# Two state products of an rwkv chain, in halves of the array's columns, and Gram products of two heads by turns

## The chip, the cores and the metric

The kernel runs on one core of one Trainium2 chip. The core has five engines: TensorE (PE, matrix products, with its weight loads shown as PEld), VectorE (DVE), ScalarE (ACT), GpSimd (POOL) and SyncE (SP, here only a DMA queue). The metric is the device time of one execution in microseconds; the lower the better. A profiled execution gives, for every instruction, when it began and how long it took.

## The reference

Two transformer-like blocks over 256 positions and 2048 channels. The second block sends one input projection through three branches (a gated delta rule "gdn", an "rwkv7" scan, an "s5" scan) and merges them. The change is in the rwkv7 branch, whose heart is this scan over positions, for 16 heads of 64 channels:

```
def step(state, xs):
    r_t, w_t, k_t, v_t, kk_t, a_t = xs
    sa = jnp.einsum('bhvk,bhk->bhv', state, -kk_t)
    state = (state * w_t[:, :, None, :] + sa[..., None] * (kk_t * a_t)[:, :, None, :]
             + v_t[..., None] * k_t[:, :, None, :])
    return state, jnp.einsum('bhvk,bhk->bhv', state, r_t)
```

## The kernel before

The big projections are float32 products, split into two parts of a shorter format (`split`, L167 and L124) and multiplied in three passes (`wh` and `wl` are the parts of the weights; the result tile is `pj`). Their weights stream from HBM through SP's queue, ACT and DVE prepare them, and PE multiplies. Nearly all of PE's time is theirs.

The rwkv scan is done in chunks of 64 positions. `rwkv` works on a group of four heads (index `q`, four groups), and each group goes through these steps:

- Gram products. For each head the products of its (64 channels x 128) operands `BK` and `KR`, both held in `G8`, for four chunks: a matrix with 64 rows (contracted) and 128 columns as weights. The heads of a pair lie on the upper and the lower 64 partitions, so on the upper and lower half of the array's rows. DVE masks the results into `U`, `W` (tile `o0`) and `E` (tile `E8`). After each head the generator yields `LAT["prod"]`.
- `inverse64`: a triangular inverse `AT` of each chunk, through two DMA round trips, DVE steps and four sets of 64x64 products (`e,d` and `c,d` in the trace), by turns on the array's upper left and lower right quarter.
- The chain over four chunks `c`. `p1` multiplies `W` with the state tile `ST` (tile `a4`: the state in its upper 64 rows, the values `v` in its lower 64), `p2` multiplies the inverse, `p3` multiplies `E` with the state; DVE and ACT carry the results from step to step. `W`'s lower right quarter (rows 64 to 127, columns 64 to 127) is zero, set by a memset on POOL.

All of this is a generator that runs beside the projections: `mm` adds an estimated time to `K.clock` for every product, and `tick`, called between the products of a projection, resumes a generator when the clock has passed its last yield (the table `LAT`, in microseconds). A second generator holds the s5 branch. Afterwards the framework's scheduler sets the final order on each engine; PE then runs strictly in the given order, so a small product whose operand is late holds up the projections behind it. The result tiles of this generator come from a ring of three PSUM buffers (`K.ps()`).

In the trace a float32 product shows as two instructions of each kind (two weight loads, two products); a projection's as one. Names are tile names without numbers: `ps<-a,o` is `p1` (moving `a4`, weights `o0`), `ps<-a,E` is `p3`, `ps<-G,AT` is `p2`, `ps<-G` are the Gram products, `ps<-s5x,ct` the read-out of the s5 branch (on 32 columns at a time), `ps<-e,bonw` a small product ahead of the Gram ones.

Of the kernel before, what the change touches and what calls it, by code (L numbers as in the profile page):

```python
# [25 lines left out]
LAT = dict(small=12.0, turn=2.5, bc=8.5, fd=10.0, fb=1.2, fh=0.8, z=0.3, sm=8.85, pt=1.42, st=6.0, ix=0.55, top=9.0, s5=11.0, inv=34.0, pr=1.3,  # L26
           prz=1.6, feat=15.0, prod=2.2, c1=1.25, c3=1.3, gn=11.0, sc=6.5, conv=22.5, ln=4.1, rw=2.3, rb=9.0, gp=1.0,
           kt=1.0, gu=3.25, gc=1.3, gR=1.5, go=1.0, gg=7.2)
# [887 lines left out]
class Block2:  # L916
# [263 lines left out]
    def rwkv(self, pl, q, f, wl, al, rn, prm, C):  # L1180
        K, nc = self.K, self.nc
# [49 lines left out]
        KR, BK = G8[:, 0], G8[:, 1]  # L1231
# [15 lines left out]
        p = K.ps()  # L1247
# [6 lines left out]
        W = K.t(self.po, [128, 4, 4, 128], "o0")  # L1254
        E = K.t(pl, [128, 4, 4, 128], "E8")
        U = K.t(pl, [128, 8, 64], "h2")
        ST = K.t(pl, [128, 4, 4, 64], "a4")
        PC = K.t(pl, [64, 4, 4], "PC")
        nc.gpsimd.memset(W[64:128, :, :, 64:128], 0.0)
        nc.gpsimd.memset(ST[0:64, 0], 0.0)  # L1260
        for j in range(2):
            nc.vector.tensor_copy(PC.rearrange("p (i j) c -> p i j c", j=2)[:, :, j], E3[64 * j:64 * j + 64, :, :, 64])
        for i in range(2):
            for j in range(2):
                h = 2 * i + j
                rows = slice(64 * j, 64 * j + 64)
                p = K.ps()
                pv = p.rearrange("p (c t) -> p c t", c=4)
                for c in range(4):
                    K.mm(pv[:, c], BK[rows, i, c].rearrange("p a t -> p (a t)"),  # L1270
                         KR[rows, i, c].rearrange("p a t -> p (a t)"))
                ms = lambda rw, m: C["ms"][rw].unsqueeze(1).to_broadcast([64, m, 64])
                lo, hi = slice(0, 64), slice(64, 128)
                for d in range(2):
                    K.tt(U[64 * d:64 * d + 64, 2 * h:2 * h + 2], pv[lo, d::2, 0:64], ms(lo, 2), ALU.mult)
                K.tt(W[hi, h, :, 0:64], pv[hi, :, 0:64], ms(hi, 4), ALU.mult)
                K.tt(E[:, h, :, 64:128], pv[:, :, 64:128], C["mi"].unsqueeze(1).to_broadcast([128, 4, 64]), ALU.mult)
                nc.scalar.copy(W[0:64, h], KR[rows, i].rearrange("p c a t -> p c (a t)"))
                yield LAT["prod"]
            p = K.ps()  # L1280
            for c in range(4):
                K.tr(p[:, c * 128:c * 128 + 128], BK[:, i, c].rearrange("p a t -> p (a t)"))
            pv = p.rearrange("p (c j n) -> p c j n", c=4, j=2)
            for j in range(2):
                nc.scalar.copy(E[:, 2 * i + j, :, 0:64], pv[:, :, j])
            p = K.ps()
            for c in range(4):
                K.tr(p[0:64, c * 128:c * 128 + 128], v[:, i, c * 64:c * 64 + 64])
            nc.scalar.copy(ST[64:128, :, 2 * i:2 * i + 2], p[0:64].rearrange("p (c j n) -> p c j n", c=4, j=2))
# [8 lines left out]
        hv = lambda p: p[:, 0:256].rearrange("p (h s) -> p h s", h=4)  # L1298
        for c in range(4):
            d = c % 2  # L1300
            rows = slice(64 * d, 64 * d + 64)
            p1 = K.ps()
            for h in range(4):
                K.mm(hv(p1)[:, h], W[:, h, c], ST[:, c, h])
            nc.vector.tensor_copy(X0[rows], hv(p1)[0:64])
            nc.scalar.copy(Y0[64:128], hv(p1)[64:128])
            if c < 3:
                pcb = PC[:, :, c:c + 1].to_broadcast([64, 4, 64])
                K.tt(mp, ST[0:64, c], pcb, ALU.mult)
            yield LAT["c1"]  # L1310
            p2 = K.ps()
            for h in range(4):
                K.mm(hv(p2)[0:64, h], AT[rows, 2 * h + c // 2], X0[rows, h])
            nc.vector.tensor_copy(ST[0:64, c], hv(p2)[0:64])
            yield LAT["c1"]
            p3 = K.ps()
            for h in range(4):
                K.mm(hv(p3)[:, h], E[:, h, c], ST[:, c, h])
            if c < 3:
                K.tt(tm, hv(p3)[0:64], pcb, ALU.mult)  # L1320
                K.tt(ST[0:64, c + 1], tm, mp, ALU.add)
            K.tt(Y[rows, c // 2], hv(p3)[64:128], Y0[64:128], ALU.add)
            yield LAT["c3"]
# [16 lines left out]
        p = K.ps()  # L1340
# [552 lines left out]
```

## Time and profile before

| what | value |
|---|---|
| time, median of 3 runs | 2163.0 us (2161.22 to 2163.57) |
| profiled execution, its own time | 2168.05 us |
| its span, first to last instruction | 2166.3 us |
| PE busy, share of the span | 2120.1 us, 98% |
| DVE, ACT, POOL busy | 77%, 48%, 2% |
| mean granted TensorE clock | 0.994 of full speed |

The profiled execution took 5.05 us longer than the median of the runs; 1.75 us of it lie outside its span. PE works nearly all the time and the other engines have room; where PE stands idle it waits for DVE or ACT. A busy PE is not PE at its peak: how close the starts of its instructions stand tells more than how long each one lasts, since they overlap.

### The profile page before, as it was taken

The numbers are of one execution on the slowest core, as the hardware profiler recorded it, in microseconds if no ns is written. First come the engines' busy times: TensorE is split into PE (matmuls) and PEld (weight loads), VectorE is DVE, ScalarE is ACT, GpSimd is POOL, SyncE is SP. The second block draws the span as 40 slices with busy tenths as digits, with TensorE's granted clock in tenths as the row PEclk, the third lists the DMA queues.
The fourth block names the chain that finished last, engine by engine and source line by source line (L and its number), as shares of the span: only waits on it lengthen the run. The fifth ranks groups of instructions, "written<-read, shape, count | busy, mean of one in ns | idle before, by whom it ended". The sixth has DMA issues, their size and how long they took to land. (4 is left out here: it accounts for less than half of the span.)

```text
span 2166.3 us, 32785 instructions
## 1 busy us (share of the span) xinstructions
PE 2120.1 (98%) x12275; PEld 1790.6 (83%) x12275; DVE 1668.8 (77%) x2919; ACT 1043.2 (48%) x1498; POOL 49.4 (2%) x113
## 2 busy tenths in 40 slices
PE   9999999999999999999999999999999999999998
PEld 8888888888898888888888788767778868888786
DVE  6788866667999876665789998988998857866565
ACT  5445454544454455555544444434446635644344
POOL 2001000000000000000000000000000000000000
PEclk9999999999999999999999999999999999999999
DMA  8666656767666766876686686676765675795674
GB/s 255 194 183 175 174 147 184 241 205 224 198 183 204 209 171 181 280 215 200 196 233 199 186 242 191 195 225 181 211 202 165 197 219 176 235 300 156 210 232 152
DMA packets 356143, 440.09 MB, mean 203 GB/s; under 512 B 50380, under 2 KB 262528, under 8 KB 355664
## 3 DMA queue, kind: packets, MB, share of 16 engines
q1 hardware_dynamic: 328240, 430.81, 65.6%
q10 hardware_dynamic: 26512, 4.68, 1.2%
q0 software_dynamic: 1232, 2.51, 0.4%
q8 instruction: 96, 1.57, 0.3%
q14 instruction: 63, 0.52, 0.1%
HBM read 396.35 MB, written 41.57 MB: 202 GB/s over the span
## 5 line engine op out<-in xcount | busy, mean ns | idle before, releaser
L167 ACT CAST wh<-raw 128x1024 fp32r<-128x1024 f32 (+4 forms) x668 | 683.8, 1026 | 860.2 <-PE pj L141 708.7
L124 DVE TENSOR_TENSOR wl<-raw,wh 128x1024 fp32r<-128x1024 f32 (+4 forms) x668 | 794.0, 1191 | 336.6 <-ACT wh L167 327.5
L141 PE MATMUL pj<-x,wh 128*128 128x512 f32 (+3 forms) x3008 | 1017.8, 387 | 0.7 <-ACT wh L167 0.7
L141 PE MATMUL pj<-x,wl 128*128 128x256 f32 (+2 forms) x2864 | 805.8, 281 | 2.3 <-DVE wl L124 2.3
L141 PEld LDWEIGHTS pj<-x,wh 128*128 128x128 f32 (+2 forms) x3008 | 553.2, 187 | 125.7 <-issue 9.1
L141 PEld LDWEIGHTS pj<-x,wl 128*128 128x128 f32 (+2 forms) x2864 | 539.1, 188 | 8.7 <-issue 4.0
L141 PE MATMUL pj<-wh,x 128*128 128x512 f32 (+2 forms) x1472 | 452.3, 383 | 0.0
L141 PEld LDWEIGHTS pj<-wh,x 128*128 128x128 f32 x1472 | 272.4, 189 | 49.0 <-issue 6.0
L141 PE MATMUL pj<-wl,x 128*128 128x512 f32 (+2 forms) x736 | 280.1, 381 | 0.9 <-DVE wl L124 0.9
L141 PEld LDWEIGHTS pj<-wl,x 128*128 128x128 f32 x736 | 139.0, 189 | 25.7 <-DVE wl L124 2.2
L141 PE MATMUL pj<-wh,y 128*128 128x512 f32 x512 | 158.3, 390 | 0.0
L141 PEld LDWEIGHTS pj<-wh,y 128*128 128x128 f32 x512 | 95.9, 188 | 19.8
L141 PE MATMUL pj<-wl,y 128*128 128x512 f32 x256 | 99.9, 390 | 0.0
L141 PE MATMUL pj<-wh,E 128*128 128x512 f32 x192 | 78.6, 409 | 2.8 <-ACT wh L167 2.3
L141 PE MATMUL pj<-wl,E 128*128 128x512 f32 x192 | 77.0, 402 | 1.9 <-DVE wl L124 1.8
L141 PE MATMUL pj<-wh,G 128*128 128x512 f32 x192 | 77.3, 403 | 0.0
L124 DVE TENSOR_TENSOR raw<-y 128x256 f32<-128x256 f32 (+7 forms) x256 | 64.0, 289 | 3.0
L141 PEld LDWEIGHTS pj<-wl,y 128*128 128x128 f32 x256 | 48.1, 188 | 9.9
L124 DVE TENSOR_TENSOR y<-raw 128x128 f32<-128x128 f32 (+7 forms) x256 | 46.2, 223 | 2.6
L141 PEld LDWEIGHTS pj<-wh,E 128*128 128x128 f32 x192 | 37.1, 193 | 12.0 <-ACT wh L167 3.2
L141 PEld LDWEIGHTS pj<-wl,E 128*128 128x128 f32 x192 | 37.0, 193 | 10.9 <-DVE wl L124 3.5
L141 PEld LDWEIGHTS pj<-wh,G 128*128 128x128 f32 x192 | 37.2, 194 | 8.0 <-issue 0.2
(457 smaller groups left out, 1997.4 us busy)
## 6 DMA issues: line engine op xcount, KB each, us to landing
raw<-in_w_in_dram SPq DMA_DIRECT2D x460, 512.0 KB, 3.8
raw<-in_w_out_dram SPq DMA_DIRECT2D x96, 512.0 KB, 4.7
raw<-in_w_branch_dram SPq DMA_DIRECT2D x48, 512.0 KB, 4.5
raw<-in_w_in_dram SPq DMA_DIRECT2D x24, 344.0 KB, 3.2
s5t<-y SPq DMA_DIRECT2D x16, 512.0 KB, 6.2
s5tb<-s5t SPq DMA_DIRECT2D x32, 256.0 KB, 3.7
raw<-in_w_in_dram SPq DMA_DIRECT2D x16, 384.0 KB, 3.6
gates<-ev SPq DMA_DIRECT2D x12, 512.0 KB, 3.7
```

The lines of the kernel that those rows point to most:

```text
L124: return (eng or self.nc.vector).tensor_tensor(out=out, in0=a, in1=b, op=op)
L141: i = self.nc.tensor.matmul(out, l, r, start=st, stop=sp, **k)
L167: i = self.nc.scalar.copy(h, src)
```

## The change

The Gram products of the two heads of a pair are now issued by turns, chunk by chunk, into two result tiles that are taken from the ring together; one yield of twice the old length follows instead of one after each head. `p1` comes as two products per head: `W`'s left 64 columns with all 128 rows, and its right 64 columns with the upper 64 rows only (the lower ones were zero; the memset is gone). `p3` comes as two products per head on the left and the right 64 columns, both with all 128 rows.

```diff
-        nc.gpsimd.memset(W[64:128, :, :, 64:128], 0.0)
         nc.gpsimd.memset(ST[0:64, 0], 0.0)
...
         for i in range(2):
-            for j in range(2):
+
+            pvs = [K.ps().rearrange("p (c t) -> p c t", c=4) for _ in range(2)]
+            for c in range(4):
+                for j, pv in enumerate(pvs):
+                    rows = slice(64 * j, 64 * j + 64)
+                    K.mm(pv[:, c], BK[rows, i, c].rearrange("p a t -> p (a t)"),
+                         KR[rows, i, c].rearrange("p a t -> p (a t)"))
+            for j, pv in enumerate(pvs):
                 h = 2 * i + j
                 rows = slice(64 * j, 64 * j + 64)
-                p = K.ps()
-                pv = p.rearrange("p (c t) -> p c t", c=4)
-                for c in range(4):
-                    K.mm(pv[:, c], BK[rows, i, c].rearrange("p a t -> p (a t)"),
-                         KR[rows, i, c].rearrange("p a t -> p (a t)"))
...
-                yield LAT["prod"]
+            yield 2 * LAT["prod"]
...
             for h in range(4):
-                K.mm(hv(p1)[:, h], W[:, h, c], ST[:, c, h])
+                K.mm(hv(p1)[0:64, h], W[:, h, c, 0:64], ST[:, c, h])
+                K.mm(hv(p1)[64:128, h], W[0:64, h, c, 64:128], ST[0:64, c, h])
...
             for h in range(4):
-                K.mm(hv(p3)[:, h], E[:, h, c], ST[:, c, h])
+                for d in (0, 64):
+                    K.mm(hv(p3)[d:d + 64, h], E[:, h, c, d:d + 64], ST[:, c, h])
```

First place: PE at the first chunk's `p1` in the first group of heads. Before (a row is one product and its count; the size is that of its output, partitions x columns):

```order
L141 MATMUL pj_11046<-x_8492,wh_11049 128x512
L141 MATMUL pj_11046<-x_8492,wl_11050 128x256
L141 MATMUL ps_1796_11062<-a_1681_10320,o_1678_10317 128x64 x4
L141 MATMUL pj_11046<-x_8492,wh_11049 128x512
L141 MATMUL pj_11046<-x_8492,wl_11050 128x256
```

and now:

```order
L141 MATMUL pj_11045<-x_8492,wh_11048 128x512
L141 MATMUL pj_11045<-x_8492,wl_11049 128x256
L141 MATMUL ps_1796_11061<-a_1681_10320,o_1678_10317 64x64 x8
L141 MATMUL pj_11045<-x_8492,wh_11048 128x512
L141 MATMUL pj_11045<-x_8492,wl_11049 128x256
```

Four products became eight in one piece with nothing between them; of the eight every second has 64 instead of 128 rows of weights, by the code above. `p3` reads the same, with `E` for `o`, and all 32 runs of `p1` and `p3` stand in one piece as here.

Second place: PE at the first Gram products, in the first group of heads. Before (`ps_1683` is the first head's result; the second head's four products follow 14 projection products later):

```order
L141 MATMUL ps_1676_10312<-e_1652_10143,bonw_10070 128x256 x2
L141 MATMUL ps_1683_10326<-G_1653_10147 128x128 x4
L141 MATMUL pj_10299<-x_8492,wh_10302 128x512
L141 MATMUL pj_10299<-x_8492,wl_10303 128x256
L141 MATMUL pj_10299<-x_8492,wh_10302 128x512
```

and now, both heads' results `ps_1683` and `ps_1684`:

```order
L141 MATMUL ps_1676_10312<-e_1652_10143,bonw_10070 128x256 x2
L141 MATMUL ps_1683_10325<-G_1653_10147 128x128
L141 MATMUL ps_1684_10326<-G_1653_10147 128x128
L141 MATMUL ps_1683_10325<-G_1653_10147 128x128
L141 MATMUL ps_1684_10326<-G_1653_10147 128x128
L141 MATMUL ps_1683_10325<-G_1653_10147 128x128
L141 MATMUL ps_1684_10326<-G_1653_10147 128x128
L141 MATMUL ps_1683_10325<-G_1653_10147 128x128
L141 MATMUL ps_1684_10326<-G_1653_10147 128x128
L141 MATMUL pj_10299<-x_8492,wh_10302 128x512
```

The second head's products moved up between the first head's.

Third place: PE at the second pair of heads in the third group (`ps_2196` and `ps_2200` are the two heads). Before:

```order
L141 MATMUL ps_2196_13341<-G_2147_13076 128x128 x4
L141 MATMUL pj_13479<-wh_13635,x_8492 128x512 x2
L141 MATMUL pj_13479<-wl_13636,x_8492 128x512
L141 MATMUL pj_13479<-wh_13635,x_8492 128x512 x2
L141 MATMUL pj_13479<-wl_13636,x_8492 128x512
L141 MATMUL pj_13479<-wh_13635,x_8492 128x512
L141 MATMUL ps_2200_13371<-G_2147_13076 128x128 x4
```

and now (`ps_2193` and `ps_2194`):

```order
L141 MATMUL ps_2192_13376<-ident_75,c_2120_13007 64x128 x4
L141 MATMUL pj_13540<-wh_13660,x_8492 128x512 x2
L141 MATMUL pj_13540<-wl_13661,x_8492 128x512
L141 MATMUL pj_13540<-wh_13660,x_8492 128x512
L141 MATMUL ps_2193_13382<-G_2144_13118 128x128 x4
L141 MATMUL pj_13540<-wh_13678,x_8492 128x512
L141 MATMUL ps_2194_13383<-G_2144_13118 128x128 x4
L141 MATMUL pj_13540<-wl_13679,x_8492 128x512
```

Here the scheduler did not keep the turns: the heads still stand apart. So it is in the second pair of the second, third and fourth group; the other five of the eight pairs stand by turns. In the first pair of those three groups the two heads' runs already stood next to each other before, one head after the other.

## Rows read from the trace of the kernel before

**Rows 1.** The page's busy time of each engine over the whole span.

```profile
PE 2120.1 (98%) x12275; PEld 1790.6 (83%) x12275; DVE 1668.8 (77%) x2919; ACT 1043.2 (48%) x1498; POOL 49.4 (2%) x113
```

**Rows 2.** Windows summed: 1130-1180, 1309-1347, 1460-1495, 1607-1648 us, where the chunk chains run.

```profile
sum 164.00, PE 163.92 PEld 137.06 DVE 139.79 ACT 70.63 POOL 3.56; mean PE 40.98 PEld 34.26 DVE 34.95 ACT 17.66 POOL 0.89
```

**Rows 3.** Groups by line and shape: rows*columns of weights, xcount | busy us, mean ns.

```profile
L141 PE MATMUL ps<-a,o 128*128 128x64 f32 x128 | 16.7, 273 | 0.1
L141 PE MATMUL ps<-G 64*128 64x128 f32 x128 | 16.7, 285 | 0.4 <-DVE E L124 0.4
L141 PE MATMUL ps<-a,E 128*128 128x64 f32 x128 | 16.1, 269 | 0.0
```

**Rows 4.** Timeline of PE at one p2 and one p1: start us, us, what.

```profile
1136.11 0.39 PE L141 MATMUL pj<-x,wh 128*128 128x512 f32 x1
1136.42 0.68 PE L141 MATMUL ps<-G,AT 64*64 64x64 f32 x8
1137.03 0.38 PE L141 MATMUL pj<-x,wl 128*128 128x256 f32 x1
1137.25 0.40 PE L141 MATMUL pj<-x,wh 128*128 128x512 f32 x1
...
1140.59 0.39 PE L141 MATMUL pj<-x,wh 128*128 128x512 f32 x1
1140.82 0.27 PE L141 MATMUL pj<-x,wl 128*128 128x256 f32 x1
1140.93 1.00 PE L141 MATMUL ps<-a,o 128*128 128x64 f32 x8
1141.74 0.47 PE L141 MATMUL pj<-x,wh 128*128 128x512 f32 x1
1142.05 0.28 PE L141 MATMUL pj<-x,wl 128*128 128x256 f32 x1
```

**Rows 5.** Timeline of PE at products of the inverse, by turns on two quarters.

```profile
1121.64 1.15 PE L141 MATMUL ps<-e,d 64*64 64x64 f32 x32
1122.72 0.50 PE L141 MATMUL pj<-x,wh 128*128 128x512 f32 x1
```

**Rows 6.** Timeline of PE where tiles of two shapes follow each other directly.

```profile
1480.06 0.62 PE L141 MATMUL ps<-s5x,ct 128*32 128x256 f32 x2
1480.61 0.67 PE L141 MATMUL ps<-G,AT 64*64 64x64 f32 x8
1481.21 1.07 PE L141 MATMUL ps<-s5x,ct 128*32 128x256 f32 x10
1482.22 0.50 PE L141 MATMUL pj<-wl,x 128*128 128x512 f32 x1
```

**Rows 7.** Timeline of PE at Gram products: one head alone, then two heads' runs adjacent.

```profile
1063.18 1.02 PE L141 MATMUL ps<-e,bonw 128*128 128x256 f32 x4
1064.13 1.16 PE L141 MATMUL ps<-G 64*128 64x128 f32 x8
1065.22 0.50 PE L141 MATMUL pj<-x,wh 128*128 128x512 f32 x1
1065.55 0.28 PE L141 MATMUL pj<-x,wl 128*128 128x256 f32 x1
...
1528.73 1.71 PE L141 MATMUL ps<-G 64*128 64x128 f32 x16
1530.37 0.50 PE L141 MATMUL pj<-wh,x 128*128 128x512 f32 x1
```

**Rows 8.** Timeline of PE in the gdn branch: last score products, first product of the inverse.

```profile
1935.06 1.02 PE L141 MATMUL ps<-E 128*128 128x256 f32 x4
1935.73 0.47 PE L141 MATMUL pj<-x,wl 128*128 128x256 f32 x1
...
1979.92 1.15 PE L141 MATMUL ps<-e,d 64*64 64x64 f32 x32 [1.06 <-DVE e L1158]
```

**Rows 9.** Windows near the end: length, busy us of each engine, granted clock.

```profile
2018.00:2036.00 18.00, 13.60 (x44) 9.72 (x43) 6.91 (x8) 6.11 (x14) 1.01 (x1) 0.81 0.72 233
```

## The prediction

> **What bounds the kernel now.** I read the page's busy line first: PE works 98% of the span, DVE 77%, POOL 2% [rows 1]. That is an average, so I then asked for the busy time in the four stretches in which the chunk chains of the four groups run (`p1`, `p2`, `p3`): PE is busy 163.92 of 164.00 us there, DVE 139.79 [rows 2]. In these stretches PE sets the pace and stands nowhere idle, so what a run of small products takes or gives back there goes into the time in full; the projections queue behind it. The groups by line say how much there is to win: `p1`, `p3` and the Gram products are 128 instructions each, 16 to 17 us of busy time each [rows 3]. More than some 20 us cannot come from making them shorter. Last, the timeline tells what one run costs, measured by when the next product starts.
>
> **Price of a run now.** `p1` is eight instructions on the whole array. A projection product with 512 columns holds PE 0.23 us (1140.59 to 1140.82), one with 256 columns 0.11 (to 1140.93), and `p1` starts with no delay. It holds PE 0.81 us, and the product behind it 0.31 instead of 0.23 [rows 4]. So 0.81 + 0.08 = 0.89 us a run, 0.11 an instruction.
>
> **Price of a run on part of the array.** `p2` is eight instructions on one 64x64 quarter. The product ahead should have ended at 1136.34, `p2` starts at 1136.42, holds PE 0.61 us, and the 256-column product behind it takes 0.22 instead of 0.11 [rows 4]: 0.08 + 0.61 + 0.11 = 0.80 us. The inverse's 32 instructions by turns on two quarters hold PE 1.08 us [rows 5]. If two run at a time they are 16 steps against `p2`'s 8, so 8 steps cost 1.08 - 0.61 = 0.47 us, 0.059 a step, and 0.14 us of a run is fixed. Not overlapped, 24 more instructions would cost 0.02 each, which nothing near it does; I take them as overlapped.
>
> What is the fixed part paid for? Where `p2` stands directly between two pieces of the s5 read-out, which uses 128x32 tiles, it still holds PE 0.60 us (1480.61 to 1481.21), and the two read-out instructions ahead 0.55 [rows 6]. So the price is not that of coming from the whole array or going back to it: a change between two shapes of tile, 64x64 and 128x32, costs 0.60 - 0.47 = 0.13 us as well. The same place shows that column groups with all 128 rows do overlap: ten 256-column instructions take 1.01 us, while on the whole array four take 0.95 [rows 6, 7].
>
> The Trainium skill has a rule for this: "Mode switching requires drain: Changing tiling mode (not just tile) drains the TensorE" (TensorEngine Tiling (Array Packing), Key Properties), and its list of modes has 128x64 and 64x64 as different ones. The rows above agree as far as they go, with 0.13 us a change; no row shows these two shapes side by side.
>
> **p1 after.** Its eight products are, head by head, one with 128 rows x 64 columns of weights and one with 64 x 64. Both halves lie on different columns, but their shapes differ, so the shape changes eight times a run. If each change costs what it costs in rows 6, a product (two instructions) takes 2 x 0.059 + 0.13 = 0.25 us, eight take 2.0, and with 0.08 ahead and 0.11 behind the run costs 2.19 us against 0.89: +1.30. There are 16 runs: +20.8 us. Bounds: if the shapes don't matter and the halves overlap, the run is 8 steps in one piece and costs `p2`'s 0.80, -0.09 x 16 = -1.4 us. If the two instructions of a product also came apart, 16 changes, 16 x 0.19 + 0.19 = 3.2 us, +37 us. I take 20.8, since `p2` between two pieces of another shape is the nearest row.
>
> **p3 after.** Both halves have 128 rows x 64 columns, one shape. By turns they are 8 steps, 0.80 us against 0.89: -0.09 x 16 = -1.4 us. If they did not overlap, 16 steps, 0.94 + 0.14 + 0.19 = 1.27, +6 us; the ten overlapping instructions of rows 6 speak against that.
>
> **Gram products after.** A head alone costs PE 1.09 us from 1064.13, 0.10 more in the product behind, and about 0.09 ahead (four 256-column instructions of about 0.215 should have ended at 1064.04): 1.28. Two heads' runs next to each other hold PE 1.64, only 0.55 more than one: the row halves do overlap once the second head's come into sight [rows 7]. By turns from the start, both heads should hold PE as one does, 1.09. In the first group two pairs save a whole run each, 2 x 1.28 = 2.6 us; in the first pair of the other groups the runs were adjacent already, 3 x 0.55 = 1.7; the second pairs of those groups are still apart (third place in the order), nothing. Sum -4.2 us; bounds 0 (no overlap) and -5 (the price ahead and behind counted again).
>
> **What I count at nothing.** The memset on POOL, which is busy 2% [rows 1]. DVE's and ACT's work on the results: the same instructions. The longer yield: the second head's results are there earlier than before. In the first group's second pair the second result tile is that of the transposes, so one head waits for two copies on ACT; 0.2 us, once.
>
> **What moves besides.** The estimated clock runs 0.64 us faster per chunk (a product with 64 output columns counts 0.107 us with 128 rows, half that with 64), and the scheduler rearranges later work. Most of it stays within a few products, but one place is larger. Before, 237 projection products stood between the last score products of the second gdn half and its inverse, and the inverse still came 1.06 us late, 44.2 us after 1935.73 [rows 8]. Now 167 stand there, 103 of 512 and 64 of 256 columns, 103 x 0.23 + 64 x 0.117 = 31.2 us: PE could wait 9 to 13 us. Against that the end of that chain comes earlier before the last branch (134 products instead of 54), where PE loses 4.4 us of 18 to waits and the granted clock falls to 0.81 [rows 9]: 6 to 8 us may come back. The first half's inverse has 180 products instead of 150, 2 to 4 us the better. I set the sum at 0, +-8.
>
> **Sum.** 20.8 - 1.4 - 4.2 + 0.2 = +15.4. PE idles 46.2 us in the whole span [rows 1], some of it behind these chains for DVE, which gains time when PE is later: I take off 2. That is +13.4 us on the profiled execution's 2168.05 (span 2166.3 and 1.75 around it), 2181.4; on the runs, whose median is 5 us lower, 2163.0 + 13.4 = 2176.
>
> **Rivals.**
> A. Shape costs nothing where the tiles touch no common part of the array. The two halves of `p1` share no column; in rows 6 the tiles may. Then -1.4 - 1.4 - 4.2 + 0.2 = -6.8 us, 2156: not slower. It decides if a run of `p1` holds PE under 0.9 us. For it: the inverse's quarters, which share neither rows nor columns, overlap fully [rows 5]. Against it: every change of shape in the rows carries the 0.13. Beside it stands a page of the Trainium skill (TensorE: Matmul & The Clock Gate, Part 3, The mechanism), by which each instruction names its row and column groups and tiles that don't conflict overlap; it would have `p1` as this rival does.
> B. As forecast, and the inverse of the second gdn half is late as well, with nothing given back at the end: +13.4 + 10 = 2186. For it: 31.2 us of work where 44.2 were needed [rows 8]. Against it: the gain behind it.
> C. The weights of the next shape are loaded while the last one still runs, so that half of the 0.13 is hidden: 8 x 0.19 + 0.19 = 1.7 a run, +13 for `p1`, +6 in all, 2169. Against it: `p2`'s first step in rows 6 hides nothing.
>
> **How the numbers follow.** Forecast 0.52, A 0.25, B 0.13, C 0.10. Runs of this kernel spread about 0.1%, so I call anything within 0.2% (4.3 us) no change: 2158.7 to 2167.3. With +-8 us of rearrangement, forecast and B are slower nearly always, C a bit over half, A faster in two of three. Slower 0.65, same 0.13, faster 0.22. The range takes in B and most of A: 2152 to 2188; the forecast's own is 2167 to 2185.
>
> **What would show it.** A `p1` run should hold PE about 2.0 us, with eight pieces 0.25 apart; a `p3` run about 0.6 with its instructions in pairs of nearly equal start; the first Gram run 16 instructions in 1.1 us; the four chain stretches together 19 us longer with the same number of projection products. It is wrong if `p1` holds PE under 1 us (rival A), or if PE's waits near the two gdn inverses differ by over 8 us from before.

## The result and the profile after

The changed kernel takes 2178.22 us (median of 4 runs, 2176.53 to 2179.41) against 2163.28 for the kernel before; the ratio is 1.0067, 95% interval 1.0052 to 1.0082. It is slower by 14.9 us, where the prediction said 13.4 and gave 2176. The profiled execution took 2179.41 us, its span is 2177.6.

The page's busy time of each engine, after:

```profile
PE 2132.2 (98%) x12531; PEld 1791.1 (82%) x12531; DVE 1670.3 (77%) x2919; ACT 1045.8 (48%) x1498; POOL 48.9 (2%) x109
```

Against [rows 1] PE is busy 12.1 us longer, with 256 more instructions, and idles 2177.6 - 2132.2 = 45.4 us instead of 46.2. So the loss is work on PE, not waiting.

The groups by line and shape, after; the columns are those of [rows 3]:

```profile
L141 PE MATMUL ps<-a,o 128*64 128x64 f32 x128 | 21.0, 246 | 0.0
L141 PE MATMUL ps<-a,o 64*64 64x64 f32 x128 | 20.8, 242 | 0.0
L141 PE MATMUL ps<-G 64*128 64x128 f32 x128 | 12.8, 284 | 1.4 <-DVE E L124 1.4
L141 PE MATMUL ps<-a,E 128*64 128x64 f32 x256 | 11.0, 228 | 0.0
```

`p1` went from 16.7 to 41.8 us of busy time, `p3` from 16.1 to 11.0, the Gram products from 16.7 to 12.8; the wait ahead of the Gram products from 0.4 to 1.4. One run of each kind in the timeline of PE, after (start us, length us, and what; neighbours in time are merged into one row):

```profile
1129.99 0.28 PE L141 MATMUL pj<-x,wl 128*128 128x256 f32 x1
1130.20 2.12 PE L141 MATMUL ps<-a,o 128*64 128x64 f32 x16
1132.25 0.50 PE L141 MATMUL pj<-x,wh 128*128 128x512 f32 x1
...
1135.86 0.28 PE L141 MATMUL pj<-x,wl 128*128 128x256 f32 x1
1136.07 0.69 PE L141 MATMUL ps<-a,E 128*64 128x64 f32 x16
1136.68 0.50 PE L141 MATMUL pj<-x,wh 128*128 128x512 f32 x1
```

The `x16` of the first run covers both shapes (the row names only the first). It holds PE 1132.25 - 1130.20 = 2.05 us: eight products, 0.256 us apart. With what it costs ahead and behind the median run takes 2.25 us, against the 0.89 of [rows 4]. `p3` has as many instructions on as many columns and holds PE 0.61 us (0.81 with both ends). Its two halves have one shape, `p1`'s have two. The first Gram products, after:

```profile
1061.98 1.02 PE L141 MATMUL ps<-e,bonw 128*128 128x256 f32 x4
1062.93 1.16 PE L141 MATMUL ps<-G 64*128 64x128 f32 x16
1064.02 0.50 PE L141 MATMUL pj<-x,wh 128*128 128x512 f32 x1
...
1070.79 1.25 PE L141 MATMUL ps<-G 64*128 64x128 f32 x16 [0.46 <-DVE E L124]
1071.97 0.39 PE L141 MATMUL pj<-x,wl 128*128 128x256 f32 x1
```

Two heads by turns hold PE 1.09 us, what one head alone took in [rows 7]. The second pair waits 0.46 us for a mask step on DVE; by the code such steps read, and so free, the result tiles of the ring.

### The profile page after: what moved, and what is told of

Same layout as the page of the kernel before. It is cut to its first block, busy times and chain, and to the rows that moved or that the text cites. A ratio compares the mean times of both kernels' runs of the same rounds, so it can differ in the third digit from the quotient of the medians.

```text
span 2177.6 us, 33290 instructions
## 1 busy us (share of the span) xinstructions
PE 2132.2 (98%) x12531; PEld 1791.1 (82%) x12531; DVE 1670.3 (77%) x2919; ACT 1045.8 (48%) x1498; POOL 48.9 (2%) x109
## 5 line engine op out<-in xcount | busy, mean ns | idle before, releaser
L141 PEld LDWEIGHTS pj<-x,wl 128*128 128x128 f32 (+2 forms) x2864 | 539.5, 188 | 12.8 <-DVE wl L124 5.6
L124 DVE TENSOR_TENSOR y<-raw 128x128 f32<-128x128 f32 (+7 forms) x256 | 46.2, 223 | 2.5
L124 DVE TENSOR_TENSOR s5w<-ps,s5tb 128x512 f32<-128x512 f32 x64 | 42.8, 684 | 2.5 <-PE ps L141 2.3
```

The lines of the kernel that those rows point to most:

```text
L124: return (eng or self.nc.vector).tensor_tensor(out=out, in0=a, in1=b, op=op)
L141: i = self.nc.tensor.matmul(out, l, r, start=st, stop=sp, **k)
```

## The experiments

PE busy and idle are those of one profiled execution; "p1 run" is the median of the runs that stand between two projection products, with the delays they cause ahead and behind. The kernel before, run beside them, took 2163.89 (median) beside the first four experiments, 2161.32 beside the next four and 2163.05 (one run) beside the last two.

| kernel | median us | ratio to before, 95% interval | p1 run us | PE busy us | PE idle us |
|---|---|---|---|---|---|
| before | 2163.28 | 1 | 0.89 | 2120.1 | 46.2 |
| after | 2178.22 | 1.0067 (1.0052 to 1.0082) | 2.25 | 2132.2 | 45.4 |
| p1 whole | 2162.89 | 1.0000 (0.9990 to 1.0011) | 0.89 | 2111.8 | 47.1 |
| p1 in one shape | 2155.64 | 0.9957 (0.9945 to 0.9969) | 0.81 | 2104.5 | 45.5 |
| p1 left, then right | 2165.50 | 1.0006 (0.9997 to 1.0015) | 1.41 | 2117.7 | 47.0 |
| p1 alone | 2183.95 | 1.0086 (1.0072 to 1.0099) | 2.25 | 2136.2 | 46.1 |
| clock count alone | 2160.62 | 0.9994 (0.9981 to 1.0007) | 0.89 | 2115.3 | 43.4 |
| Gram alone | 2165.82 | 1.0005 (0.9991 to 1.0018) | 0.89 | 2111.8 | 44.9 |
| p3 alone | 2168.64 | 1.0028 (1.0016 to 1.0040) | 0.89 | 2123.1 | 52.3 |
| one shape, and a pause | 2146.55 | 0.9923 (0.9907 to 0.9938) | 0.81 | 2101.8 | 44.4 |
| disjoint, two shapes | 2181.72 (1 run) | | 2.23 | 2134.8 | 45.1 |
| disjoint, one shape | 2157.45 (1 run) | | 0.81 | 2109.7 | 46.0 |

**p1 whole again.** In the changed kernel:

```diff
-                K.mm(hv(p1)[0:64, h], W[:, h, c, 0:64], ST[:, c, h])
-                K.mm(hv(p1)[64:128, h], W[0:64, h, c, 64:128], ST[0:64, c, h])
+                K.mm(hv(p1)[:, h], W[:, h, c], ST[:, c, h])
```

> The changed kernel with p1 on the whole array again (and the memset of W's zero quarter back); p3 and the Gram products stay changed. Main theory (a change between the tile shapes 128x64 and 64x64 costs about 0.13 us, eight times a p1 run): the whole loss goes, a p1 run costs 0.89 us again, the sum is 2163 - 1.4 (p3) - 4.2 (Gram) = 2157, with 8 us either way for the rearrangement of the later work. Rival R (the loss is the rearrangement of work around the inverses, p1 is a bystander): 2170 or more.

The loss is gone (0.9990 to 1.0011), so `p1` made it and rival R fell. But the 5.6 us that `p3` and the Gram products should have brought don't show either; 2162.9 lies inside the 8 us allowed, at its far side.

**p1 in two products of one shape.**

```diff
-                K.mm(hv(p1)[0:64, h], W[:, h, c, 0:64], ST[:, c, h])
-                K.mm(hv(p1)[64:128, h], W[0:64, h, c, 64:128], ST[0:64, c, h])
+                for d in (0, 64):
+                    K.mm(hv(p1)[d:d + 64, h], W[:, h, c, d:d + 64], ST[:, c, h])
```

> The changed kernel with p1 still in two products a head by turns, but both with all 128 rows (the lower rows of the right half are zero again, by the memset), so that all have the shape 128x64. Main theory (the price is the change of shape): a run becomes eight steps in pairs like p3, 0.80 us instead of 2.25, and the time is 2163 - 1.4 - 1.4 - 4.2 = 2156, 8 us either way. Rival D (the price is that of more, smaller products by turns on two column halves, whatever their shape): a run stays near 2.2 us and the time at 2178. Rival R (rearrangement): 2170 or more.

2155.64, as the main theory said. The number of products and the columns they use are the changed kernel's; the right halves have 64 rows of zeros more. Its run in the timeline of PE:

```profile
1127.66 0.28 PE L141 MATMUL pj<-x,wl 128*128 128x256 f32 x1
1127.87 0.69 PE L141 MATMUL ps<-a,o 128*64 128x64 f32 x16
1128.48 0.50 PE L141 MATMUL pj<-x,wh 128*128 128x512 f32 x1
```

0.61 us on PE instead of 2.05, by doing more arithmetic. Rival D fell: turns and halves cost nothing by themselves. The stretch from the first `p1` to behind the last `p3` of the first group of heads, which holds 180 projection products before, after and with one shape, says the same in windows (columns: length, then busy us and count for PE, PEld, DVE, ACT and POOL, granted clock, DMA share, GB/s). Before, after, and with one shape:

```profile
1133.82:1179.19 45.37, 45.37 (x302) 38.30 (x301) 39.04 (x65) 18.66 (x27) 0.95 (x1) 1.00 0.69 206
```

```profile
1130.20:1180.78 50.58, 50.58 (x366) 39.51 (x365) 39.28 (x66) 18.77 (x27) 0.00 (x0) 1.00 0.60 178
```

```profile
1127.87:1172.76 44.89, 44.89 (x365) 35.63 (x364) 39.01 (x66) 18.65 (x27) 0.95 (x1) 1.00 0.69 202
```

The last two are 5.69 us apart, four runs of 2.25 - 0.81 = 1.44 (5.8). From before to after it is +5.21, where a quarter of the forecast 19 is 4.75; in the other three groups the number of projection products changed, so the forecast can't be read there. PE stands nowhere idle in any of the three, so all of it counts. The later work of the kernel with one shape stands in another order than the changed kernel's (237 projection products ahead of the second gdn inverse, as before, not 167), so its time alone would not settle the cause; the next kernel's does.

**p1's left products, then its right ones.**

```diff
                 K.mm(hv(p1)[0:64, h], W[:, h, c, 0:64], ST[:, c, h])
+            for h in range(4):
                 K.mm(hv(p1)[64:128, h], W[0:64, h, c, 64:128], ST[0:64, c, h])
```

> The changed kernel with the same eight products of p1 in another order: the four with 128 rows first, then the four with 64 rows, so one change of shape inside a run instead of seven, but no turns. Main theory: 16 steps of 0.059 us, one change of 0.13 and 0.13 + 0.19 at the ends make 1.40 us a run, 0.5 us over before: 16 x 0.5 = 8, less 1.4 and 4.2 = 2166, 8 us either way. Rival E (each 64-row product has a price of its own, 0.13 us, whichever product stands ahead of it): half of the seven prices is not saved, a run stays at 1.9 us or more, 2174 or more.

2165.50 and 1.41 us a run: the dose fits. Over the 0.81 of a run in one shape by turns, this one has eight steps more that don't overlap (8 x 0.058 = 0.47) and one change of shape, which leaves 0.13 to 0.14; the changed kernel has seven changes, (2.25 - 0.81 - 0.47) / 7 = 0.14. Rival E (a price of the 64-row products) fell. This kernel also keeps the changed kernel's order at the gdn inverses (180 and 167 projection products ahead of them), so the two differ in `p1`'s runs: 16 x (2.25 - 1.41) = 13.4 us by the runs, 12.7 by the medians.

**p1 alone.** The kernel before with `p1`'s two lines as in the changed kernel.

> The kernel before with p1 alone changed (memset gone); Gram products and p3 as before. Main theory: 16 runs at 2.25 instead of 0.89 us, +21.7: 2184, 6 us either way. Rival R (rearrangement is what counts): under 2172.

2183.95, 20.1 us above the kernel before it was run beside; 16 x 1.36 = 21.8 by the runs of `p1`. `p1` alone makes the whole loss and more, and rival R fell again.

**Clock count alone.** The kernel before, whose products are only counted as dearer:

```diff
                 K.mm(hv(p1)[:, h], W[:, h, c], ST[:, c, h])
+                K.clock += 160 / 3
...
                 K.mm(hv(p3)[:, h], E[:, h, c], ST[:, c, h])
+                K.clock += 320 / 3
```

> The kernel before, with no instruction changed, but p1 and p3 counted in the estimated clock as the change counts them (0.64 us more per chunk), so that only the order of the later work moves. My prediction put the rearrangement at 0, 8 us either way. Theory: 2163, at most 4 us either way, since no run of small products costs another amount; the sum of PE's waits moves by no more than that. Rival R (order alone is worth what the change cost): 2172 or more.

No difference (0.9981 to 1.0007). Its order is not the changed kernel's, though: 237 projection products still stand ahead of the second gdn inverse, so it shows what this much clock moves, and not what the change moved. Yet PE's busy time in the profile differs by 4.8 us from the first profile's with not one instruction changed; two profiled executions cannot tell a few microseconds. The granted clock is one reason: its mean was 0.996 here and 0.994 there, and 0.002 of the span is 4.3 us, an estimate of the most that it can make.

**The Gram change alone.** The kernel before with the changed kernel's Gram loop and its one yield.

> The kernel before with the Gram change alone (by turns, one longer yield); p1 and p3 as before. By my sum -4.2: 2159. Rival W (what the turns save in PE comes back as waits, as PE is blocked by the first step behind the later result, seen in the kernel with p1 whole again, where PE waited some 4 us more than before): 2163.

1.0005 (0.9991 to 1.0018) excludes the -4.2. The twelve runs fall into two groups, four from 2155.99 to 2158.82 and eight from 2163.63 to 2167.07; in the shortest the mean granted clock was 0.996, in the longest 0.992. The profile is of an execution of 2158.82, of the first group, so it doesn't show where the others lost. Rival W's number (no change) was met; its cause was not shown.

**p3 alone.**

```diff
-                K.mm(hv(p3)[:, h], E[:, h, c], ST[:, c, h])
+                for d in (0, 64):
+                    K.mm(hv(p3)[d:d + 64, h], E[:, h, c, d:d + 64], ST[:, c, h])
```

> The kernel before with p3 alone changed. A p3 run costs 0.81 us instead of 0.90: 16 x -0.09 = -1.4, so 2161.8, 4 us either way for the rearrangement. Rival W (the order of the later work decides, not the runs): any value outside 2158 to 2166.

My expectation failed: 1.0028 (1.0016 to 1.0040) is slower, 6 us, though a run of `p3` fell from 0.89 to 0.81 as it should. In the profile PE idles 6.1 us more than in [rows 1]. The two long waits in its timeline of PE, in the gdn branch some 600 us behind the first `p3`, in the longest of its twelve runs:

```profile
1755.58 0.79 PE L141 MATMUL pj<-wl,E 128*128 128x512 f32 x1 [5.16 <-DVE wl L124]
...
1777.09 1.97 PE L141 MATMUL ps<-e,d 64*64 64x64 f32 x32 [7.36 <-DVE e L1158]
```

The second is the first gdn half's inverse, which waited 3.45 us before. The granted clock was lower as well over the twelve runs: 0.990 to 0.994, in the mean 0.9926, against 0.993 to 0.998 and 0.9953 in the kernel before beside them. The 0.0027 between the means are 5.8 us of the span, an estimate of the most that the clock can make, and about the whole loss. So what cost lies outside the runs of `p3`. That the order of the later work made the waits, and the waits the lower clock, is a reading; no run here takes them apart.

**One shape, and a pause before the second pair of heads.** The kernel with `p1` in one shape, and:

```diff
         for i in range(2):
+            if i:
+                yield LAT["prod"]
             pvs = [K.ps().rearrange("p (c t) -> p c t", c=4) for _ in range(2)]
```

> The changed kernel with p1's halves in one shape (as in the run with one shape, 2155.6) and a pause of the generator ahead of the Gram products of the second pair of heads, so that seven of the eight pairs stand by turns instead of five. Two pairs more save one run each, 1.3 us: 2155.6 - 2.6 = 2153, 4 us either way. Rival W (the waits take it back): 2156 or more.

2146.55: faster than the kernel before by 0.8% (0.9907 to 0.9938), and the best of all. Seven of the eight pairs stand by turns; the group of Gram products:

```profile
L141 PE MATMUL ps<-G 64*128 64x128 f32 x128 | 10.4, 285 | 0.3 <-DVE E L124 0.3
```

Without the pause it was 12.8 us of busy time and 1.5 of waiting: 3.6 us by the rows, a little over the 2.6 expected, and the two profiled spans differ by 3.8. The medians differ by 9.1, the ratios by 0.34% (7.4 us); the other kernel was profiled in its shortest run (2151.81). Its runs had a mean granted clock of 0.9944, those of the best kernel 0.9960, which by the same estimate makes 3.4 us at most; what made the rest is not shown.

**The price by itself.** `p1` cut to tiles that share neither rows nor columns of the array, once in two shapes, once in one. Both kernels leave out a part of the sums and serve only to measure:

```diff
-                K.mm(hv(p1)[0:64, h], W[:, h, c, 0:64], ST[:, c, h])
-                K.mm(hv(p1)[64:128, h], W[0:64, h, c, 64:128], ST[0:64, c, h])
+                K.mm(hv(p1)[0:64, h], W[0:64, h, c, 0:64], ST[0:64, c, h])
+                K.mm(hv(p1)[64:128, h], W[64:96, h, c, 64:128], ST[64:96, c, h])
```

> A measurement of the price by itself. The changed kernel with p1 cut to tiles that share neither rows nor columns of the array, by turns: rows 0 to 63 of W with the left 64 columns (shape 64x64), rows 64 to 95 with the right 64 columns (shape 32x64). This leaves out the products of the values in the left half and of the state in the right half, so the output is not the reference's. Main theory (the shape as such costs, wherever the tile lies): eight pieces a run 0.25 us apart, a run costs 2.2 us as in the changed kernel. Rival A (only tiles that touch a common part wait for each other): pairs of nearly equal start, 0.8 us a run.

The control has `64:128` in place of `64:96`:

> The control of the run before it: p1 cut to tiles of one shape that share neither rows nor columns, by turns: rows 0 to 63 with the left 64 columns, rows 64 to 127 with the right 64 columns (both 64x64). It leaves out the same kind of products (the values in the left half, the state in the right one). Both theories: eight steps in pairs of nearly equal start, 0.8 us a run, as the inverse on two quarters.

A run in the timeline of PE, first with two shapes (64x64 and 32x64), then with one:

```profile
1130.65 2.10 PE L141 MATMUL ps<-a,o 64*64 64x64 f32 x16
1132.69 0.50 PE L141 MATMUL pj<-x,wh 128*128 128x512 f32 x1
```

```profile
1129.92 0.68 PE L141 MATMUL ps<-a,o 64*64 64x64 f32 x16
1130.53 0.50 PE L141 MATMUL pj<-x,wh 128*128 128x512 f32 x1
```

2.04 us against 0.61, with the same number of products. The first has less arithmetic than the second and takes over three times as long. Both have the changed kernel's order at the gdn inverses, and their times, one run each, are 24.3 us apart, 16 x (2.23 - 0.81) = 22.7 by the runs. Rival A of the prediction fell in its own form: tiles that touch no common part wait for each other as well, when their shapes differ.

## Why the prediction was right, and where it was not

**p1, +20.8: right.** Eight pieces 0.25 apart were forecast, 0.256 came; 2.25 - 0.89 = 1.36 us a run, x 16 = +21.8. A change costs 0.14, not 0.13. The rule of the Trainium skill that a change of tiling mode drains the TensorE (TensorEngine Tiling (Array Packing), Key Properties) agrees with every run here, at 0.14 us a change. The other page of the Trainium skill, beside which rival A stood (TensorE: Matmul & The Clock Gate, Part 3), says that tiles which don't conflict overlap; in these runs that holds only within one shape (0.61 us a run of sixteen instructions, 2.04 with two shapes). Rival C (half of the price hidden) asked for 0.19 a piece; 0.256 was measured.

**p3, -1.4: right for the run** (0.81 instead of 0.89), though alone the edit made the kernel 6 us slower, in work and waits outside these runs.

**Gram, -4.2 and +0.2 of waiting: a size was off.** The busy time of the group fell by 3.9, but the waits ahead of it grew by 1.0 (0.4 to 1.4). I had counted 0.2, once, for two copies on ACT in the first group's second pair; PE waits there 0.46 us, for a mask step on DVE, and the wait ahead of the last head of the fourth group grew from 0.16 to 0.62. Net -2.9.

**Rearrangement, 0 with 8 either way: the sum held, the steps under it failed.** PE's idle time changed by -0.8. But I had said that the second gdn half's inverse would wait 9 to 13 us; it waited 3.0, and 2.0 more fell on two projection products ahead of it that waited for a weight part (`wl`). And that the first half's would be 2 to 4 us the better; it went from 3.45 to 6.73. That these and the gain at the end cancel is luck in part, since their sizes were wrong. PE at the first half's inverse before, then at both after (the bracket is the wait just ahead, and what ended it):

```profile
1755.13 1.97 PE L141 MATMUL ps<-e,d 64*64 64x64 f32 x32 [3.45 <-DVE e L1158]
```

```profile
1758.41 0.39 PE L141 MATMUL pj<-wl,E 128*128 128x512 f32 x1
1765.53 1.97 PE L141 MATMUL ps<-e,d 64*64 64x64 f32 x32 [6.73 <-DVE e L1158]
...
1968.75 1.15 PE L141 MATMUL ps<-e,d 64*64 64x64 f32 x32 [3.01 <-DVE e L1158]
```

The step that failed took the 44.2 us of [rows 8] as the length of the chain and put PE's work beside it. It is no constant. With 167 projection products between the last score products and the inverse, the second half's chain took 37.4 us (1931.31 to 1968.75), and 35.2 with `p1` whole; with 237 it took 43.1 to 46.4 in the kernels where that count was kept. DVE runs the chain's steps in one order with its other steps, and some of those wait for PE's products, so fewer products ahead may let the chain come sooner; that is a reading, no run isolates it.

The first half's chain grew from 40.2 us (1714.91 to 1755.13) to 44.8 (1720.73 to 1765.53) though PE had 30 products more to cover it. Its last part is a round trip through two transfers. Issue of the transfers on ACT's queue and the DVE step that needs the second, after:

```profile
1750.41 0.58 ACTq L1145 DMA_DIRECT2D dim<-b  x1
1753.05 0.60 ACTq L1148 DMA_DIRECT2D e<-dim  x1
...
1753.80 0.61 ACTq L1148 DMA_DIRECT2D e<-dim  x1
1764.76 0.71 DVE L1158 STREAM_TRANSPOSE e<-e 128x512 f32<-128x512 f32 x1 [6.79 <-DMA e<-dim]
```

and in the best kernel, where PE didn't wait there at all:

```profile
1728.96 0.58 ACTq L1145 DMA_DIRECT2D dim<-b  x1
1734.18 0.60 ACTq L1148 DMA_DIRECT2D e<-dim  x1
...
1734.90 0.60 ACTq L1148 DMA_DIRECT2D e<-dim  x1
1740.51 0.70 DVE L1158 STREAM_TRANSPOSE e<-e 128x512 f32<-128x512 f32 x1
```

From the last issue to the step it is 10.96 us after, 6.65 before, 5.6 in the best kernel. The whole round trip in windows (the last two columns are DMA share and GB/s), before, after and in the best kernel:

```profile
1742.70:1754.37 11.67, 7.95 (x33) 5.61 (x31) 6.03 (x7) 4.94 (x5) 0.12 (x1) 1.00 0.97 286
```

```profile
1750.32:1764.76 14.44, 8.47 (x38) 6.69 (x36) 6.13 (x7) 5.17 (x5) 0.12 (x1) 0.90 0.91 267
```

```profile
1728.87:1740.51 11.64, 10.48 (x44) 7.87 (x43) 6.91 (x8) 4.40 (x5) 0.12 (x1) 1.00 1.00 297
```

So 2.8 of the 4.6 us by which the chain grew are in this round trip. The DMA engines were as busy in the short trips as in the long one, so their busy share does not tell the two apart. Whether the transfers of weights on SP's queue, now in other places, hold these back no run here tried; it stays open.

**The end of the last branch: right.** The stalls of [rows 9] are gone; behind 1998 us PE waits nowhere. The 4.4 us of waits came back, and with the granted clock at 1.00 instead of 0.81 of 18 us at most 3.4 more (an estimate), so 4.4 to 7.8 where I had 6 to 8. Rival B (a late inverse and nothing given back) fell. The window after:

```profile
2018.00:2036.00 18.00, 18.00 (x83) 14.70 (x82) 12.19 (x12) 8.89 (x9) 0.00 (x0) 1.00 0.63 190
```

**The sum.** By the rows 21.8 - 1.4 - 3.9 is +16.5 of busy time, and the page shows +12.1. The 4.4 us between them are in other stretches, of the size by which the profile of the kernel with the clock count alone differed from the first one without any change of work. The execution profiled before also lies 5 us over its median, so the two profiled spans are 11.3 us apart where the medians are 14.9. I had taken off 2 us for waits absorbed; that was a guess, and nothing here confirms it. That the total came within 1.5 us is therefore luck in part: with the waits, the three terms make 21.8 - 1.4 - 2.9 = +17.5, and what took 2.6 us off again is not shown.

## What to carry to other kernels

A small product's price on a busy TensorE is read from the start of the next product, and lies in the change of tile shape more than in its rows or columns: order products so that equal shapes stand together, and fill a smaller tile with zeros to the shape of its neighbour where that saves a change. Before splitting a product by turns, make both halves the same shape. A few microseconds saved in a run of products need not show in the time when the order of later work moves with the edit (`p3` alone, Gram alone): time each edit alone, with enough runs, and look at the longest waits far behind it and at the granted clock of every run.

## What the runs showed of the hardware that I had not expected

- The 0.14 us of a change falls in two parts: inside a piece the second instruction starts 0.107 us behind the first instead of 0.058, so 0.049; the other 0.091 stand ahead of the piece (0.149 from its predecessor's last start). In `p3`, whose instructions start in pairs 0.006 us apart, the second pair starts 0.107 us behind the first in the same way, and the later ones 0.058.
- The price doesn't ask whether tiles are disjoint: 64x64 and 32x64 on different rows and columns pay it in full (2.04 against 0.61 us for sixteen instructions).
- A long wait costs PE more than its length. The inverse's 32 instructions took 1.97 us behind the wait of 6.73, with the granted clock at half of full speed (1.2 GHz), and 1.97 behind that of 3.45 before. Behind that of 3.01 they took 1.15, but the price only came later: the granted clock fell some 1.4 us after the wait, and the next 32 instructions took 1.97. In the best kernel, without a wait, the first half's 32 took 1.15. Behind the wait of 6.73 the clock rose again within 4 us. Windows of the kernel after, from that wait on; then, behind the wait of 3.01, the next 32 instructions and a window in them:

```profile
1757.00:1765.50 8.50, 1.79 (x8) 1.14 (x7) 1.72 (x3) 1.72 (x2) 0.00 (x0) 0.79 1.05 334
1765.50:1767.40 1.90, 1.88 (x32) 1.79 (x32) 1.08 (x1) 0.00 (x0) 0.00 (x0) 0.50 0.16 63
1767.40:1769.40 2.00, 2.00 (x14) 1.42 (x14) 0.00 (x0) 0.59 (x1) 0.00 (x0) 0.66 0.68 167
1769.40:1772.00 2.60, 2.60 (x44) 1.98 (x40) 0.00 (x0) 0.66 (x2) 0.00 (x0) 1.00 1.00 357
```

```profile
1971.17 1.97 PE L141 MATMUL ps<-e,d 64*64 64x64 f32 x32
```

```profile
1971.00:1972.00 1.00, 1.00 (x17) 0.83 (x18) 0.66 (x1) 0.00 (x0) 0.00 (x0) 0.50 0.79 190
```
